# A two-layer hybrid trunk on one core: norms moved into a matmul group, a branch tile run ahead, and a re-laid end

## The chip, the core and the metric

The kernel runs on one core of a Trainium2 chip. The metric is the device time of one execution in microseconds (us); less is better. The median of the runs shown is 905.42 us (905.33 to 906.95, three runs).

Engines have short names, as in the profile: PE is TensorE (PEld its weight loads), DVE is VectorE, ACT is ScalarE, POOL is GpSimd, SP is the engine that only issues DMAs here. ACT issues some DMAs too. SPq and ACTq are the queues of these issues.

## The reference, cut to what matters

1024 prompt tokens and 32 tokens of a second stream go through two layers of width 1024. Layer 0 is a gated recurrence over 1408 channels, layer 1 a windowed attention, and each adds its normed output to its input:

```python
def rglru_block(x, ...):                      # layer 0
    u = rmsnorm(x, norm_pre) @ w_in           # 1024 -> 2 x 1408
    branch, gate = u[..., :D_RNN], u[..., D_RNN:]
    conv = conv_b + sum of four taps of branch along the tokens
    xb = conv in 16 blocks of 88 channels
    r = sigmoid(xb @ w_r + b_r)               # block-diagonal, 88 x 88
    i = sigmoid(xb @ w_i + b_i)
    h = recurrence(a(r), b(r, i, conv))       # along the tokens
    y = (h * silu(gate)) @ w_out
    return x + rmsnorm(y, norm_post)
k, v = shared_kv(x)                           # from the output of layer 0
def swa_block(x, k, v, ...):                  # layer 1
    u = rmsnorm(x, norm_pre) @ w_in           # queries and a gate
    o = windowed attention with sinks(q, k, v)
    y = (o * silu(gate)) @ w_out
    return x + rmsnorm(y, norm_post)
```

The outputs are y of both streams, the last rows of the convolution, the last states of the recurrence, and the K and V rows. The order of sums and the fp32 accuracy matter to the kernel only in that it computes every product of two fp32 matrices from halves, as follows.

## The kernel before, in words

**Products.** Every fp32 operand of a matmul is split into a high part (rounded to the matmul's format fp32r) and a low part (what is left). `split` (L112 to L117) makes them: ACT copies the high part (L116), and VectorE subtracts it (L117); for some weights GpSimd subtracts. `mm3` (L146 to L152) computes a product as three matmuls for each 128 rows of the inner dimension: high weights by high data (L150), high by low (L151), low by high (L152). An inner dimension of 1024 is thus a group of 24 matmuls, all added up in one PSUM bank. `mm3_steps` (L698) is the same as a generator that hands the control back every six matmuls, so that other work can be traced between. A bank holds 512 fp32 columns; eight banks go round.

**Tokens.** All tokens stand along the free dimension, 1060 columns with three columns of gap between the streams, in three chunks `NSA`: 0 to 384, 384 to 768, 768 to 1060. Channels stand along the 128 partitions: the 1408 branch channels are 11 tiles `br0` to `br10`.

**The front.** x arrives chunk by chunk. The first NS = 3 branch tiles are run chunk by chunk as well (`first_mm`, L310): tiles 0, 1, 2 of chunk 0, then of chunk 1, then of chunk 2 (loop at L328). `branch_mm` multiplies with x unnormed; the factor 1/rms of each token comes later. `x_stat(n)` makes it for three token tiles: ACT squares rows of x, small operations finish the root, and VectorE writes it on the diagonal of a 128 x 128 matrix `diag` (L289). `x_norm(n)` (L291 to L306) multiplies these by a matrix of ones (L296, banks `rs0` to `rs2`), which puts the factors on all partitions, and ACT copies them to `rs` (L299). Then come `branch_evac` (L207: VectorE, `ext` = bank times `rs`), and `branch_conv`: ACT does the first tap (L222), VectorE three more (L224, one operation each), and the result is split to `chi` and `clo`. In the loop, `x_norm(0)` is called behind tile 1 of chunk 1 and `x_norm(1)` behind tile 0 of chunk 2; `x_norm(2)` follows the loop.

**Branch and gates.** The loop at L445 goes over the branch tiles from 3 on: `branch_mm(t)` for all three chunks, `branch_evac`, the next weights, `branch_conv`, and then `gates` of an earlier tile by the table `GATES_AT`: gate 0 stands behind branch tile 3, gate 1 behind tile 4, and so on. A gate product (bank `gt<tile>_<gate>_<chunk>`) has the tile's own 128 channels and a few rows of its neighbours, since blocks of 88 channels cross the tiles. These rows are packed into a tile `pack` by DMAs (`pack_rows`, L371; half of them issued by SP, half by ACT), and each bank's group is closed by two matmuls with them (L390, L391). `weights` loads weight tiles through four buffers `raw` and splits them into six buffers each of `whi` and `wlo`.

**The order.** The program is traced as written, and a scheduler then orders each engine's instructions by a simulated time and by priorities. `urgent()` raises the priority of what is traced in it. `pin` keeps an instruction behind the one that was traced before it on the same engine; what isn't pinned may be moved ahead. A tile's buffers come free when the last reader has run, and the next load into the same buffer waits for that.

**The end.** `out_b(1)` projects the last-but-one group of tokens (416 columns, `OUT[1]`) onto eight tiles of channels, banks `obm0_1` to `obm7_1`. Each bank is read twice by ACT: the square `qp` (L614), which GpSimd adds to a running sum (L616), and the copy `zb`. When the eighth is added, `rsqrt_of` (L158, bank `ss_p`) multiplies the sum by ones on TensorE, and `post_norm` normalises the eight `zb` tiles on VectorE (L601), adds the residuals `res` (loaded by SP in 16 DMAs, L580; the addition is L607), and SP stores them. Meanwhile `prep_t(c, k)` (L1095 to L1104) loads and splits the sixteen weight tiles of the last product, `t<c>_<k>`: c is the half of the output channels, k the 128 rows of the inner dimension. They go through the same four `raw` buffers. `T_AT` places t0_0 to t0_7 and t1_6, t1_7 into `out_b(1)` (split to `wth`, `wtl`); t1_0 to t1_5 are traced at the start of `out_t` (split to `wthi`, `wtlo`, for they take the ring's buffers `whi`, `wlo`).

`out_t` (L1106 to L1149) computes the last 256 tokens the other way round: tokens on partitions, 512 output channels in a bank. There are four tiles in the order (c, t) = (0, 0), (0, 1), (1, 0), (1, 1), banks `ot<t>_<c>`, 24 matmuls each. For each ACT squares the bank with a running sum (`junk`, L1134) and VectorE multiplies the bank by the gain into `zt` (L1137). When both halves of a token tile are there, TensorE transposes the residual into the banks `xt` (L1125), a few operations on one column finish the root, VectorE does `zt` times root plus `xt` for each half (L1147), and two DMAs store them, the first issued by SP, the second by ACT. The loop at L1159 runs `out_t` and, behind each of its steps, one step of `norm_b(1)`, which is the norm of the eight `zb` tiles.

## Time and profile before

| what | before |
|---|---|
| median of the runs | 905.42 us (905.33 to 906.95) |
| the profiled execution's own time | 905.81 us |
| its span in the profile | 904.0 us |
| mean granted TensorE clock | 0.995 |
| PE busy from 0 to 75 us | 69.70 us, clock 0.98 |
| PE busy from 75 to 862 us | 782.14 of 787 us, clock 1.00 |
| PE busy from 862 to 890 us | 25.79 of 28 us, clock 0.94 |
| PE busy from 890 to 904 us | 7.72 of 14 us, clock 0.91 |

The profile is that of one execution; times in it count from the span's start. A row of a timeline gives start and length in us, the engine, the line, the operation with its tiles, shapes, how many of a kind follow each other (x6), and in brackets the idle time before it and what ended it. "PEclk" and the clock in a row of stretches are the TensorE clock that the chip granted, as a share of the full one. Durations of single matmuls overlap each other, so the cost of one is read from the distance between starts.

### The profile page before, as it was taken

The page shows a single profiled execution, that of the slowest core. Times are in us where ns is not written, and L with a number is a line of the kernel's source. Part 1 is how long each engine was busy: PE and PEld are TensorE (multiplying, and loading weights), DVE is VectorE, ACT ScalarE, POOL GpSimd, SP SyncE. Part 2 cuts the span into 40 slices and gives each one's busy share as a digit, 9 for nine tenths or more (in the row PEclk, how much of TensorE's full clock was granted, in tenths as well). Part 3 has the DMA queues.
Part 4 walks back from the last instruction along what each step waited for, and adds up shares of the span by engine and source line. Part 5 has one row for each costly group of instructions (what it writes and reads, how often), then busy time and mean ns, then how long its engine had stood idle before and what let it go on. Part 6 is the DMA issues. An engine that isn't in the chain of part 4 may idle for free. (4 is left out here: it accounts for less than half of the span.)

```text
span 904.0 us, 15787 instructions
## 1 busy us (share of the span) xinstructions
PE 885.4 (98%) x5434; PEld 864.4 (96%) x5434; DVE 708.1 (78%) x1499; ACT 563.1 (62%) x1231; POOL 221.7 (25%) x263
## 2 busy tenths in 40 slices
PE   9989999999999999999999999999999999999997
PEld 8989999999999999999989899999999999999975
DVE  6797878878897654177897847999999989998776
ACT  8748877879454325364663527766767757797661
POOL 5250212114300001126362432122122011202330
PEclk9999999999999999999999999999999999999999
DMA  9522433242533216445545667338338338334884
GB/s 337 204 75 77 135 88 125 81 128 92 181 119 124 89 57 190 146 135 178 163 157 186 210 205 205 98 111 231 96 110 239 103 97 239 121 112 160 281 250 144
DMA packets 95777, 137.35 MB, mean 152 GB/s; under 512 B 16144, under 2 KB 64304, under 8 KB 95696
## 3 DMA queue, kind: packets, MB, share of 16 engines
q1 hardware_dynamic: 86040, 123.30, 43.9%
q10 hardware_dynamic: 9480, 12.49, 4.5%
q8 instruction: 43, 0.70, 0.3%
q0 software_dynamic: 176, 0.54, 0.2%
q14 instruction: 38, 0.31, 0.1%
HBM read 99.28 MB, written 32.13 MB: 145 GB/s over the span
## 5 line engine op out<-in xcount | busy, mean ns | idle before, releaser
L150 PE MATMUL oa<-yh,whi_outa 128*128 128x384 f32 (+1 forms) x264 | 85.8, 326 | 0.0
L151 PE MATMUL gb<-xlo,whi_ina 128*128 128x384 f32 (+1 forms) x264 | 85.6, 324 | 0.0
L152 PE MATMUL gb<-xhi,wlo_ina 128*128 128x384 f32 (+1 forms) x264 | 85.4, 323 | 0.0
L150 PE MATMUL gb<-xhi,whi_ina 128*128 128x384 f32 (+1 forms) x264 | 85.2, 323 | 0.0
L151 PE MATMUL oa<-yl,whi_outa 128*128 128x384 f32 (+1 forms) x264 | 85.1, 323 | 0.0
L152 PE MATMUL oa<-yh,wlo_outa 128*128 128x384 f32 (+1 forms) x264 | 85.1, 323 | 0.0
L616 POOL TENSOR_TENSOR qp<-qp,qp 128x384 f32<-128x384 f32 (+2 forms) x34 | 49.3, 1449 | 138.2 <-ACT qp L614 126.5
L150 PE MATMUL br<-xhi,whi_ina 128*128 128x384 f32 (+1 forms) x240 | 77.8, 324 | 0.0
L151 PE MATMUL br<-xlo,whi_ina 128*128 128x384 f32 (+1 forms) x240 | 77.8, 324 | 0.0
L152 PE MATMUL br<-xhi,wlo_ina 128*128 128x384 f32 (+1 forms) x240 | 77.4, 323 | 0.0
L117 DVE TENSOR_TENSOR wlo_outa<-raw_outa,whi_outa 128x512 fp32r<-128x512 f32 (+1 forms) x60 | 43.7, 742 | 42.7 <-ACT whi_outa L116 42.6
L931 ACT ACTIVATE P<-P,sm 128x257 f32<-128x257 f32 (+1 forms) x132 | 64.3, 490 | 8.0 <-DVE sm L928 7.9
L698 PE MATMUL gB<-xl,whi_g 128*128 128x384 f32 (+1 forms) x192 | 63.0, 328 | 0.0
L698 PE MATMUL gB<-xh,whi_g 128*128 128x384 f32 (+1 forms) x192 | 62.9, 328 | 0.0
L698 PE MATMUL gB<-xh,wlo_g 128*128 128x384 f32 (+1 forms) x192 | 62.6, 326 | 0.0
L116 ACT ACTIVATE whi_outa<-raw_outa 128x512 fp32r<-128x512 f32 (+1 forms) x60 | 35.5, 594 | 41.5 <-PE oa L151 25.1
L224 DVE SCALAR_TENSOR_TENSOR conv<-ext,pa,conv 128x1060 f32<-128x1060 f32 (+2 forms) x51 | 50.2, 1005 | 9.0 <-ACT conv L222 8.6
L928 DVE CUSTOM_DVE_ANT_0 P<-S,mask,nsnk 128x256 f32<-128x256 f32 (+1 forms) x128 | 52.8, 463 | 4.9 <-PE S L926 4.8
L151 PEld LDWEIGHTS oa<-yl,whi_outa 128*128 128x128 f32 x264 | 49.6, 188 | 0.4
L150 PEld LDWEIGHTS oa<-yh,whi_outa 128*128 128x128 f32 x264 | 49.6, 188 | 0.4
L150 PEld LDWEIGHTS gb<-xhi,whi_ina 128*128 128x128 f32 x264 | 49.7, 188 | 0.0
L152 PEld LDWEIGHTS oa<-yh,wlo_outa 128*128 128x128 f32 x264 | 49.7, 188 | 0.0
(301 smaller groups left out, 2894.0 us busy)
## 6 DMA issues: line engine op xcount, KB each, us to landing
raw_ina<-w_in_a SPq DMA_DIRECT2D x44, 256.0 KB, 2.8
raw_outa<-w_out_a SPq DMA_DIRECT2D x40, 256.0 KB, 2.7
raw_ob<-w_out_b SPq DMA_DIRECT2D x32, 256.0 KB, 2.6
qscr<-quadq SPq DMA_DIRECT2D x8, 768.0 KB
Q<-qscr SPq DMA_DIRECT2D x32, 192.0 KB, 4.3
hscr<-u SPq DMA_DIRECT2D x11, 530.0 KB, 3.0
xr<-xr SPq DMA_DIRECT2D x8, 512.0 KB, 10.2
raw_g<-w_in_b SPq DMA_DIRECT2D x16, 256.0 KB, 3.3
```

What stands on the lines that cost most here:

```text
L116: pin(S.activation(dst_hi, src, AF.Copy), behind)
L117: (lo_eng or V).tensor_tensor(dst_lo, src, dst_hi.bitcast(F32), op=ALU.subtract)
L150: nc.tensor.matmul(ps, wh, xh, start=i == 0, stop=False)
L151: nc.tensor.matmul(ps, wh, xl, start=False, stop=False)
L152: nc.tensor.matmul(ps, wl, xh, start=False, stop=last and i == n - 1)
L224: V.scalar_tensor_tensor(c, e[:, c0 + k:c1 + k], pa[:, t, k:k + 1], c, op0=ALU.mult, op1=ALU.add)
L616: G.tensor_tensor(sums[0], sums[0], q, op=ALU.add)
L698: nc.tensor.matmul(ps, l, r, start=c == 0, stop=c == 3 * n - 1)
L928: V.tensor_tensor_reduce(pt[:, h, :w], sb[:, (h - h0) * 256:(h - h0) * 256 + w], msk, -0.125, nsnk[:, sk][:, h:h + 1], op0=ALU.add, op1=AL ...
L931: S.activation(pt[:, h, :w + 1], pt[:, h, :w + 1], AF.Exp, bias=nmax[:, h:h + 1], scale=-1.0, accum_out=rsum[:, h:h + 1])
```

## The change

It has five parts.

1. `mm3` gets two more arguments. `mid` is called when half of the groups' steps have been traced, and the matmul behind it is pinned; `behind` pins the first matmul. `branch_mm` and `first_mm` pass both on. In the front's loop `x_norm(n - 1)` is now called in the middle of the tile behind which it stood (tile 1 of chunk 1, tile 0 of chunk 2), and the first matmul of the tile that follows is pinned.
2. At t = 3, chunks 0 and 1 of branch tile 4 are multiplied and evacuated ahead of gate 0; at t = 4 only its chunk 2 is left.
3. In `prep_t` the split of the second half's weights (c = 1) is pinned on ACT behind what was traced before it.
4. The last tile of `out_t` (c = 1, t = 1) is computed in two half banks of 256 columns, each with its own square and gain; the first half's sum (`s2`) is added into `s0`.
5. The loop over `out_t` leaves out the step of `norm_b(1)` behind the first step of `out_t`.

```diff
-    def mm3(ps, ws, xs, last=True):
+    def mm3(ps, ws, xs, last=True, mid=None, behind=False):
         n = len(ws)
         for i, ((wh, wl), (xh, xl)) in enumerate(zip(ws, xs)):
-            nc.tensor.matmul(ps, wh, xh, start=i == 0, stop=False)
+            if mid and i == n // 2:
+                mid()
+            pin(nc.tensor.matmul(ps, wh, xh, start=i == 0, stop=False), behind and i == 0 or mid and i == n // 2)
...
     for n in (1, 2):
         for m in range(NS):
-            first_mm(n, m)
-            if m == 2 - n:
-                x_norm(n - 1)
+            first_mm(n, m, (lambda: x_norm(n - 1)) if m == 2 - n else None, m == 3 - n)
...
     for t in range(MR):
         if t >= NS:
-            branch_evac(t, branch_mm(t))
+            branch_evac(t, branch_mm(t, (2,) if t == 4 else (0, 1, 2)))
         wts.pop(t)
         if t >= NS - 2:
             prep_in(t + 2)
+        if t == 3:
+            branch_evac(4, branch_mm(4, (0, 1)))
...
-        split(*wt[c, k], raw)
+        split(*wt[c, k], raw, behind=c == 1)
...
         for c in range(2):
             for t in range(2):
...
+                s0, s1, ms, y, r, s2 = (sm[:, t, i:i + 1] for i in range(6))
+                parts = [(0, 256, s2), (256, 512, s1)] if c and t else [(0, 512, s1 if c else s0)]
+                for a, b, acc in parts:
+                    ps = bank(f"ot{t}_{c}_{a}")[:, :b - a]
+                    yield from mm3_steps(ps, [tuple(x[:, t * P:(t + 1) * P] for x in oghl[k, 2]) for k in range(KD)],
+                                         [tuple(x[:, a:b] for x in wt[c, k]) for k in range(KD)])
+                    junk = fin_tile(f"junk{t}_{c}_{a}", b - a, "junk", bufs=1)
+                    S.activation(junk, ps, AF.Square, accum_out=acc)
+                    if c == 0:
+                        V.tensor_scalar(s0, s0, 1.0 / 1024.0, EPS, op0=ALU.mult, op1=ALU.add)
+                    V.tensor_tensor(zt[t][:, c * 512 + a:c * 512 + b], ps, gpost[:, c * 512 + a:c * 512 + b], op=ALU.mult)
+                    if acc is s2:
+                        V.scalar_tensor_tensor(s0, s2, 1.0 / 1024.0, s0, op0=ALU.mult, op1=ALU.add)
...
-    for _ in out_t():
-        next(nb, None)
+    for i, _ in enumerate(out_t()):
+        if i:
+            next(nb, None)
```

How these parts move instructions in the engines' queues is shown at three places. A row of the order has the line, the operation, the tile written, the tiles read, the shape, how many alike follow each other, and in some lists the semaphores waited for. Lines below L146 of before are two to nine further down in the changed kernel.

The first place is TensorE's queue in the front, before: `br1_1` is tile 1 of chunk 1, `br2_1` tile 2 of chunk 1, `rs0` the bank of the first norm.

```order
L152 MATMUL br1_1_376<-xhi6_98,wlo_ina1_4_194 128x384
L150 MATMUL br1_1_376<-xhi7_99,whi_ina1_4_193 128x384
L151 MATMUL br1_1_376<-xlo7_107,whi_ina1_4_193 128x384
L152 MATMUL br1_1_376<-xhi7_99,wlo_ina1_4_194 128x384
L296 MATMUL rs0_401<-diag_141,ones_66 128x128
L150 MATMUL br2_1_436<-xhi0_92,whi_ina2_0_226 128x384
L151 MATMUL br2_1_436<-xlo0_100,whi_ina2_0_226 128x384
L152 MATMUL br2_1_436<-xhi0_92,wlo_ina2_0_227 128x384
L150 MATMUL br2_1_436<-xhi1_93,whi_ina2_0_226 128x384
L296 MATMUL rs0_401<-diag_141,ones_66 128x128 x2
```

The same place in the changed kernel:

```order
L152 MATMUL br1_1_376<-xhi3_95,whi_ina1_0_187 128x384
L153 MATMUL br1_1_376<-xlo3_103,whi_ina1_0_187 128x384
L154 MATMUL br1_1_376<-xhi3_95,wlo_ina1_0_188 128x384
L298 MATMUL rs0_389<-diag_141,ones_66 128x128 x3
L152 MATMUL br1_1_376<-xhi4_96,whi_ina1_4_193 128x384
```

All three matmuls of `rs0` stand together now, twelve matmuls ahead of the end of tile 1, where the first of them stood.

The second place is TensorE's queue where gate 0 begins, before (`br3_2` is the last chunk of branch tile 3, `gt0_0_2` is gate 0's first half, chunk 2):

```order
L151 MATMUL br3_2_736<-xlo7_107,whi_ina3_4_648 128x292
L152 MATMUL br3_2_736<-xhi7_99,wlo_ina3_4_649 128x292
L150 MATMUL gt0_0_0_799<-chi0_410,whi_gate0_0_654 128x384
L151 MATMUL gt0_0_0_799<-clo0_411,whi_gate0_0_654 128x384
L152 MATMUL gt0_0_0_799<-chi0_410,wlo_gate0_0_655 128x384
L150 MATMUL gt0_0_1_806<-chi0_410,whi_gate0_0_654 128x384
L151 MATMUL gt0_0_1_806<-clo0_411,whi_gate0_0_654 128x384
L152 MATMUL gt0_0_1_806<-chi0_410,wlo_gate0_0_655 128x384
L150 MATMUL gt0_0_2_813<-chi0_410,whi_gate0_0_654 128x292
L150 MATMUL gt0_1_0_821<-chi0_410,whi_gate0_0_654 128x384
```

And in the changed kernel (`br4_1` is chunk 1 of branch tile 4, `pack0` the packed rows):

```order
L152 MATMUL br4_1_803<-xhi7_99,whi_ina4_4_669 128x384
L153 MATMUL br4_1_803<-xlo7_107,whi_ina4_4_669 128x384
L154 MATMUL br4_1_803<-xhi7_99,wlo_ina4_4_670 128x384
L152 MATMUL gt0_0_0_853<-chi0_398,whi_gate0_0_654 128x384
L153 MATMUL gt0_0_0_853<-clo0_399,whi_gate0_0_654 128x384
L154 MATMUL gt0_0_0_853<-chi0_398,wlo_gate0_0_655 128x384
L390 MATMUL gt0_0_0_853<-pack0_658,whi_gate0_0_654 128x384
L391 MATMUL gt0_0_0_853<-pack0_658,wlo_gate0_0_655 128x384
```

The 48 matmuls of `br4_0` and `br4_1` stand ahead of gate 0, and the packed rows are asked for behind three matmuls of it; before, the scheduler had put matmuls of other banks ahead of the packed rows, the one that waits for chunk 2 (`gt0_0_2`) among them.

The third place is the end. ACT's queue around the last square, before (`qp4_1_7` is the square of the eighth bank, `wth1_7` and `wthi1_0` to `wthi1_4` are splits of the last weights; a name in the waits is a semaphore: DMAHW4 is signalled by a load):

```order
L116 ACTIVATE wth1_7_10677<-raw_t1_7_10675 128x512 [waits DMAHW7_49]
L614 ACTIVATE qp4_1_6_10623<-obm6_1_10597 128x416 [waits PE_49,Pool_49]
L1045 ACTIVATE zb6_1_10622<-obm6_1_10597,gains_82 128x416 [waits DVE_49]
L116 ACTIVATE wthi1_0_10720<-raw_t1_0_10718 128x512 [waits DMAHW0_49]
L116 ACTIVATE wthi1_1_10726<-raw_t1_1_10724 128x512 [waits DMAHW2_49]
L116 ACTIVATE wthi1_2_10732<-raw_t1_2_10730 128x512 [waits DMAHW3_49,DVE_49]
L116 ACTIVATE wthi1_3_10738<-raw_t1_3_10736 128x512 [waits DMAHW4_49,DVE_49]
L614 ACTIVATE qp4_1_7_10665<-obm7_1_10639 128x416 [waits PE_49]
```

ACT's queue in the changed kernel:

```order
L616 ACTIVATE qp4_1_6_10623<-obm6_1_10597 128x416 [waits PE_49,Pool_49]
L1047 ACTIVATE zb6_1_10622<-obm6_1_10597,gains_82 128x416 [waits DVE_49]
L116 ACTIVATE wthi1_0_10720<-raw_t1_0_10718 128x512 [waits DMAHW0_49]
L116 ACTIVATE wthi1_1_10726<-raw_t1_1_10724 128x512 [waits DMAHW2_49]
L116 ACTIVATE wthi1_2_10732<-raw_t1_2_10730 128x512 [waits DMAHW3_49,DVE_49]
L616 ACTIVATE qp4_1_7_10665<-obm7_1_10639 128x416 [waits PE_49]
L1047 ACTIVATE zb7_1_10664<-obm7_1_10639,gains_82 128x416
L116 ACTIVATE wth1_6_10671<-raw_t1_6_10669 128x512 [waits DMAHW4_49]
L116 ACTIVATE wth1_7_10677<-raw_t1_7_10675 128x512 [waits DMAHW7_49]
L116 ACTIVATE wthi1_3_10738<-raw_t1_3_10736 128x512 [waits DMAHW4_49,DVE_49]
```

The splits of t1_6, t1_7 and t1_3 have gone behind the last square; those of t1_0, t1_1 and t1_2 have not.

SP's queue at the same place, before (`raw_t1_2` is the load of weight tile t1_2, `res4_1_0` the first residual):

```order
L1098 DMA raw_t1_1_10724<-w_out_t 128x512 [waits DMAHW2_49,DVE_49]
L1098 DMA raw_t1_2_10730<-w_out_t 128x512 [waits DMAHW4_49,DMAHW3_49,DVE_49]
L1098 DMA raw_t1_3_10736<-w_out_t 128x512 [waits DMAHW7_49,DVE_49]
L1098 DMA raw_t1_4_10742<-w_out_t 128x512 [waits DMAHW5_49,DMAHW0_49,DVE_49]
L1098 DMA raw_t1_5_10748<-w_out_t 128x512 [waits DMAHW6_49,DMAHW2_49,DVE_49]
L580 DMA res4_1_0_10681<-x1scr_3742 128x384
```

SP's queue in the changed kernel:

```order
L1100 DMA raw_t1_2_10730<-w_out_t 128x512 [waits DMAHW3_49,DMAHW0_49,DVE_49]
L1100 DMA raw_t1_3_10736<-w_out_t 128x512 [waits DMAHW4_49,DMAHW2_49,DVE_49]
L582 DMA res4_1_0_10681<-x1scr_3742 128x384 [waits DMAHW5_49]
...
L582 DMA res4_1_7_10688<-x1scr_3742 128x32 [waits DMAHW4_49]
L1100 DMA raw_t1_4_10742<-w_out_t 128x512 [waits DMAHW5_49,DVE_49]
L1100 DMA raw_t1_5_10748<-w_out_t 128x512 [waits DMAHW6_49,DVE_49]
L1059 DMA o_y<-zb0_1_10250 128x416 [waits DMAHW7_49,DVE_49]
```

The load of t1_2 waits for DMAHW0 in place of DMAHW4, which the load of t1_0 and that of t1_6 signal: it takes the buffer that t1_0 frees, where it took t1_6's. The loads of t1_4 and t1_5 have gone behind the sixteen residual loads. On ACT's queue the store of the first token tile's second half (`o_yt` from `zt0`) now stands ahead of the last square.

More of the change, by code (lines that the diff above doesn't have):

```diff
@@ L189, in _trunk, with branch_mm @@
     conv, chl, ext, gw, pack = {}, {}, {}, {}, {}
-    def branch_mm(t, ns=(0, 1, 2)):
+    def branch_mm(t, ns=(0, 1, 2), mid=None, behind=False):
         if t not in ext:
@@ L198, in branch_mm @@
             ps = bank(f"br{t}_{n}")
-            mm3(ps[:, :c1 - c0], wts[t], x_of(c0, c1))
+            mm3(ps[:, :c1 - c0], wts[t], x_of(c0, c1), mid=mid, behind=behind)
             banks.append((n, ps))
@@ L308, in _trunk, with first_mm @@
     open_ = {0: [], 1: [], 2: []}
-    def first_mm(n, m):
+    def first_mm(n, m, mid=None, behind=False):
         if n == 0 and m:
             prep_in(m)
-        open_[n].append(branch_mm(m, (n,)))
+        open_[n].append(branch_mm(m, (n,), mid, behind))
     x_split(0)
@@ L1128, in out_t @@
             for t in range(2):
-                ps = bank(f"ot{t}_{c}")
-                yield from mm3_steps(ps, [tuple(x[:, t * P:(t + 1) * P] for x in oghl[k, 2]) for k in range(KD)],
-                                     [wt[c, k] for k in range(KD)])
-                junk = fin_tile(f"junk{t}_{c}", 512, "junk", bufs=1)
-                s0, s1, ms, y, r = (sm[:, t, i:i + 1] for i in range(5))
-                S.activation(junk, ps, AF.Square, accum_out=s1 if c else s0)
-                if c == 0:
-                    V.tensor_scalar(s0, s0, 1.0 / 1024.0, EPS, op0=ALU.mult, op1=ALU.add)
-                V.tensor_tensor(zt[t][:, c * 512:(c + 1) * 512], ps, gpost[:, c * 512:(c + 1) * 512], op=ALU.mult)
+                s0, s1, ms, y, r, s2 = (sm[:, t, i:i + 1] for i in range(6))
[11 more added lines that the diff above has]
+                        V.scalar_tensor_tensor(s0, s2, 1.0 / 1024.0, s0, op0=ALU.mult, op1=ALU.add)
                 if c == 1:
```

## The prediction

> **What bounds the kernel now.** I read the page first: the engine shares, then TensorE's waits, then its stretches and its timeline at the two long waits.
>
> ```profile
> span 904.0 us, 15787 instructions
> PE 885.4 (98%) x5434; PEld 864.4 (96%) x5434; DVE 708.1 (78%) x1499; ACT 563.1 (62%) x1231; POOL 221.7 (25%) x263
> ```
>
> TensorE is the bound: 904.0 - 885.4 = 18.6 us is all the time that a reordering can win from its idle time. The change removes no matmul, so I look for where those 18.6 us lie.
>
> ```profile
> PE gt L150 <- ACT chi L116: 3.6, 1, 3.6
> PE ss_p L158 <- POOL qp L616: 2.2, 1, 2.2
> PE rAk L698 <- DVE xl L117: 1.8, 2, 1.3
> ```
>
> The two longest single waits are one in the front (a gate matmul waits for the split of the third chunk, 3.6 us) and one at the end (the ones-matmul ss_p waits for the last sum of squares, 2.2 us). The change touches both. The stretches show what such a wait costs besides itself (columns: start and end, length, busy time of PE, PEld, DVE, ACT, POOL, then TensorE's granted clock, DMA share, GB/s).
>
> ```profile
> 60.00:65.00 5.00, 2.81 (x9) 2.81 (x10) 5.00 (x11) 1.79 (x4) 3.12 (x2) 0.67 0.30 84
> 500.00:600.00 100.00, 96.83 (x625) 93.76 (x624) 76.24 (x204) 54.82 (x153) 30.84 (x32) 1.00 0.51 156
> 878.00:880.00 2.00, 2.00 (x6) 1.57 (x5) 1.97 (x5) 0.77 (x3) 0.00 (x0) 0.50 0.84 234
> ```
>
> After the 3.6 us wait and after the 2.2 us wait the granted clock was low (0.67, 0.50); in the stretch that holds the 1.3 us wait it was 1.00. So a wait of 2.2 us or more is paid twice, one of 1.3 us once.
>
> **The front.** TensorE's timeline (start, length):
>
> ```profile
> 29.64 0.38 PE L296 MATMUL rs<-diag,ones 128*128 128x128 f32 x2
> ...
> 44.84 0.94 PE L296 MATMUL rs<-diag,ones 128*128 128x128 f32 x6
> ...
> 57.38 0.33 PE L150 MATMUL gt<-chi,whi_gate 128*128 128x384 f32 x1
> ...
> 58.26 0.33 PE L152 MATMUL gt<-chi,wlo_gate 128*128 128x384 f32 x1
> 62.19 0.93 PE L150 MATMUL gt<-chi,whi_gate 128*128 128x292 f32 x2 [3.60 <-ACT chi L116]
> ...
> 65.47 0.34 PE L150 MATMUL br<-xhi,whi_ina 128*128 128x384 f32 x1
> ...
> 70.51 0.34 PE L152 MATMUL br<-xhi,wlo_ina 128*128 128x384 f32 x1
> 70.97 0.41 PE L390 MATMUL gt<-pack,whi_gate 96*128 96x384 f32 x1
> ```
>
> One 384-column matmul takes (58.26 - 57.38) / 5 = 0.176 us from start to start, one of 292 columns by its columns 0.134. The stretch loses three things: 62.19 - 58.26 - 0.176 = 3.75 us of standing; then the six matmuls of 384 and six of 292 columns from 62.19 to 65.47 take 3.28 us where 6 x 0.176 + 6 x 0.134 = 1.86 would do, so 1.42 us of low clock; and 70.97 - 70.51 - 0.176 = 0.28 us for the packed rows. Together 5.45 us, the most that the front can win.
>
> Now 48 matmuls of branch tile 4 (two chunks of 384) stand ahead of the first gate matmul: 48 x 0.176 = 8.4 us of work that needs only x and weights that were split by 50 us. Gate 0 then starts at 57.38 + 8.4 = 65.8. What it waited for must be ready by then. These are the engines that feed it:
>
> ```profile
> 25.48 0.68 DVE L289 TENSOR_SCALAR diag<-ident,stat 128x128 f32<-128x128 f32 x3
> ...
> 31.73 1.49 DVE L207 TENSOR_TENSOR ext<-br,rs 128x384 f32<-128x384 f32 x3 [1.82 <-ACT rs L299]
> ...
> 44.08 4.28 DVE L224 SCALAR_TENSOR_TENSOR conv<-ext,pa,conv 128x384 f32<-128x384 f32 x4
> ...
> 49.85 2.73 DVE L224 SCALAR_TENSOR_TENSOR conv<-ext,pa,conv 128x384 f32<-128x384 f32 x5
> ...
> 62.92 1.19 DVE L117 TENSOR_TENSOR clo<-conv,chi 128x292 fp32r<-128x292 f32 x3
> ```
> ```profile
> 44.57 1.28 POOL L117 TENSOR_TENSOR wlo_ina<-raw_ina,whi_ina 128x512 fp32r<-128x512 f32 x1 [2.23 <-ACT whi_ina L116]
> ```
> ```profile
> 63.39 2.83 SPq L371 DMA_DIRECT2D pack<-clo  x3
> ```
> ```profile
> DMA to landing us min/median/max: 6.5/6.5/6.5
> ```
>
> The splits end at 62.92 + 1.19 = 64.1 already today, 1.7 us before 65.8, so the 3.75 us and their 1.42 us of low clock go even if VectorE gains nothing. The packed rows are the next thing late: 63.39 is their issue, about 64.4 that of tile 1's part, and with 6.5 us to landing they came at 70.9, just when TensorE took them. In the new order TensorE wants them after three matmuls of gate 0, at 65.8 + 0.5 = 66.3. With the old issue it would stand 70.9 - 66.3 = 4.6 us there.
>
> ```profile
> 31.20 0.49 ACT L299 ACTIVATE rs<-rs 128x384 f32<-128x384 f32 x1 [1.50 <-PE rs L296]
> ```
>
> So the other front edit carries weight: x_norm(0) in the middle of a tile. The three rs matmuls stood in two pieces, the first behind tile 1; now all three stand twelve matmuls earlier, at 29.64 - 12 x 0.176 = 27.5. Their input is there at 25.48 + 0.68 = 26.2, so the pin makes no wait. With some 0.6 us for the three (0.94 for three at 44.84) and ACT's 0.49 they let VectorE's ext start near 28.7, which is 3.0 us sooner than 31.73, and VectorE was idle then. How much of it lasts? Its convs take 4.28 / 4 = 1.07 us each beside POOL's weight splits and 2.73 / 5 = 0.55 without, and convs moved forward meet more of POOL's splits. Bounds: nothing lasts (0), or 5 us do (chunk 1's norm comes forward too). I take 3.3, near the 3 of the start. Then the packed rows land at 70.9 - 3.3 = 67.6, less the 0.4 below: TensorE stands 0.9 us, inside the range that costs no clock. The whole-bank norms of chunk 2 at 44.84 are pinned as before and need a diag that VectorE now makes among those slow convs; I put 0.4 us for it (0 to 1). It delays everything behind it, gate 0 too, which is why it comes off the landing's lateness.
>
> The front: 5.45 - 0.4 - 0.9 + about 0.2 for the fewer changes between rs and branch matmuls = 4.4 us won; range 5.4 to 2.0. Branch 4's last chunk needs the bank of its first, which VectorE frees behind the first conv of tile 3, some 4 us before TensorE asks. From 75 us on TensorE shows no wait for hundreds of us and ACT's work after gate 0 shifts as well, so I let the gain stand to the end.
>
> **The end.** ACT, POOL, TensorE, VectorE and the DMA queue at the 2.2 us wait:
>
> ```profile
> 872.09 1.70 ACT L116 ACTIVATE wthi<-raw_t 128x512 fp32r<-128x512 f32 x3
> 874.65 0.63 ACT L116 ACTIVATE wthi<-raw_t 128x512 fp32r<-128x512 f32 x1 [0.86 <-DMA raw_t<-w_out_t]
> 875.18 0.50 ACT L614 ACTIVATE qp<-obm 128x416 f32<-128x416 f32 x1
> ```
> ```profile
> 875.82 1.10 POOL L616 TENSOR_TENSOR qp<-qp,qp 128x416 f32<-128x416 f32 x1 [2.85 <-ACT qp L614]
> ```
> ```profile
> 871.33 0.69 DVE L117 TENSOR_TENSOR wtl<-raw_t,wth 128x512 fp32r<-128x512 f32 x1 [1.08 <-ACT wth L116]
> ```
> ```profile
> 874.52 7.54 SPq L580 DMA_DIRECT2D res<-x1scr  x16
> ```
>
> The last square (875.18) stands behind a weight split that waits for its load. That load (t1_3) could start only when VectorE had split t1_7 and freed its buffer, 871.33 + 0.69 = 872.0, and took until 874.65: 2.6 us. The pin moves the splits of t1_6 and t1_7 behind the square, but those of t1_0, t1_1 and t1_2 stay ahead, as the order shows, and t1_2 now takes t1_0's buffer. So the square waits for t1_0's landing, its two splits, and t1_2's load. t1_0 is issued right behind t1_7, which landed near 870.7 (VectorE's split at 871.33 follows ACT's 0.63 us one), and it was there by 872.09; I take 871.2 (bounds 870.7 and 872.1). Splits 0.63 + 0.69 give 872.6, the load 2.6 gives 875.2, the split about 0.55 until the next starts: the square at 875.7, 0.5 us later than now (bounds 0 and 1.4). The wait for ss_p does not go; it grows by about 0.5, less 0.2 for the two transposes that stand ahead of it now.
>
> The loads t1_4 and t1_5 fall behind the sixteen residual loads.
>
> ```profile
> res<-x1scr SPq DMA_DIRECT2D x6, 192.0 KB, 2.9
> ```
> ```profile
> 887.74 0.40 PE L698 MATMUL ot<-wthi,ogh 128*128 128x512 f32 x1
> ```
> ```profile
> 880.82 1.09 DVE L601 TENSOR_TENSOR zb<-zb,r 128x416 f32<-128x416 f32 x2
> ...
> 890.16 1.09 DVE L607 TENSOR_TENSOR zb<-zb,res 128x416 f32<-128x416 f32 x2
> ```
>
> SP starts the residuals about 0.8 us sooner (t1_3 waits for t1_1's splits, near 873.3), so t1_4 is issued near 873.7 + 7.54 = 881.3 and lands with about 3 us, as the residuals do (2.9), at 884.4. Split, it is ready at 884.4 + 0.63 + 0.69 = 885.7. TensorE takes it at 887.74 now and some 0.4 us later then, so it has 2.4 us of cover. But VectorE's zb work stands behind that split, in order. Its first three operations would be done near 883.4 (1 us later than from 880.82), it idles until 885.0, and it has two splits to do there (1.4 us). Its list, done at 890.16 + 1.09 = 891.2 now, is done near 893.4. From there the tail follows:
>
> ```profile
> 896.89 0.60 ACT L1134 ACTIVATE junk<-ot 128x512 f32<-128x512 f32 x1 [4.80 <-DMA o_yt<-zt]
> ...
> 897.61 0.69 DVE L1137 TENSOR_TENSOR zt<-ot,gpost 128x512 f32<-128x512 f32 x1 [2.72 <-ACT junk L1134]
> ...
> 899.29 1.41 DVE L1147 SCALAR_TENSOR_TENSOR zt<-zt,smt,xt 128x512 f32<-128x512 f32 x2
> ```
>
> ```profile
> L117 DVE TENSOR_TENSOR ogl<-ogr,ogh 128x256 fp32r<-128x256 f32 x6 | 2.5, 416 | 0.0
> ```
>
> With half a bank last, the square and the gain after the last matmul shrink as a 256-column operation does (0.42 us against 0.69): some 0.25 us each, 0.5 won. The 48 half-width matmuls cost what 24 cost, by columns. But tile 0's output DMA on ACT's queue now stands ahead of the last square and waits for VectorE, which comes late: I put 0.6 lost (0 to 2). The end: +0.3 - 0.5 + 0.6 = 0.4 us lost; range 0.7 won to 2 lost.
>
> **Sum.** The profiled execution took 905.81 us (904.0 of span). 905.81 - 4.4 + 0.4 = 901.8. The median of the runs, 905.42, lies 0.39 below, so I predict 901.4 for a median. A difference under 0.2% (1.8 us) can't be told from none.
>
> **The rule weighed.** Row: the 2.2 us wait was followed by a granted clock of 0.50. The Trainium skill, "TensorE: Matmul & The Clock Gate", "Why this matters for your kernels", says to leave no idle gap over about 3 us between bursts. By that rule a 2.2 us gap would keep the clock. This trace disagrees (0.50 in the row), and the measurement decides. It matters for the first rival, where a pack wait of 2.2 to 3 us is paid with the low clock by the rows; by the page's rule its time would be 1.4 us less, 903.8.
>
> **Rivals.**
> - *The packed rows take the wait's place* (or the gain is given back in a later wait for VectorE). For it: 4.6 us of lateness if VectorE gains nothing. Against: its 1.82 us idle before ext. With 3 us of wait the low clock returns: 5.45 - 0.4 - 3.0 - 1.4 = 0.6 won, 0.4 lost at the end: 905.2 as a median.
> - *The end's wait does go*, if t1_2's load comes early. For it: 2.2 and about 1.4 us of clock are there. Against: the square still stands behind t1_2. 901.4 - 3.6 = 897.8.
> - *Slower: t1_4 lands late behind the residual loads.* Each us of lateness goes through VectorE's list to the end, and past 2.4 us TensorE stands too. A full queue is in this profile:
>
> ```profile
> xr<-xr SPq DMA_DIRECT2D x8, 512.0 KB, 10.2
> ```
>
>  With 10.2 instead of 3 us: 7.2 later, 908.6. It decides for slower from 4.0 + 1.8 = 5.8 us of lateness. Against: the residual loads' own landing is near 3.
>
> **How the numbers follow.** Forecast 0.63, packed rows or given back 0.20, end's wait goes 0.10, late t1_4 0.07. The forecast's bounds, front and end both best or both worst, are 905.4 - 5.4 - 0.7 = 899.3 and 905.4 - 2.0 + 2.0 = 905.4; the first rival's 905.2 belongs inside. So 899.0 to 905.6 leaves out the second rival and the third, 0.17. Faster by over 0.2% is below 903.6: 0.61 of the forecast and the 0.10, so 0.71. Within: 0.02 and nearly all of the 0.20, 0.21. Slower: 0.07 and a little, 0.08.
>
> **What would show it.** Right: no wait at gt0 near 62; rs near 27.5; a wait under 1.3 us at the first pack matmul; clock 1.00 there; the ss_p wait still 2 us or more with its low clock; the last square right behind tile 0's output DMA. Wrong: a pack wait over 2 us, an ss_p without wait, VectorE waiting past 888 for t1_4.

## The result, and the profile after

The changed kernel takes 901.35 us (median of 11 runs, 900.23 to 905.13), the kernel before, run beside it, 905.94 us (11 runs). The ratio is 0.9950, with a 95% interval of 0.9936 to 0.9964: faster by 3.3 to 5.8 us. The forecast was 901.4 us.

The profiled execution of the changed kernel is a long one, 903.26 us. First the head of its page, then TensorE's waits in the front and at the end (in all, times, longest).

```profile
span 901.5 us, 15838 instructions
PE 881.8 (98%) x5458; PEld 863.3 (96%) x5458; DVE 704.3 (78%) x1501; ACT 563.9 (63%) x1233; POOL 214.0 (24%) x263
```
```profile
PE br L152 <- ACT xhi L120: 1.5, 2, 0.8
...
PE rs L298 <- DVE diag L291: 0.3, 1, 0.3
```
```profile
PE ss_p L160 <- POOL qp L618: 1.4, 1, 1.4
```

The 3.6 us wait of the gate matmul is gone, a wait of 0.3 us at the norms of chunk 2 is new, and the ss_p wait is 1.4 us instead of 2.2. The stretches of the changed kernel, in the same columns as before:

```profile
60.00:65.00 5.00, 5.00 (x31) 5.00 (x30) 2.68 (x7) 3.07 (x5) 3.04 (x5) 1.00 0.63 149
65.00:70.00 5.00, 5.00 (x32) 5.00 (x31) 4.23 (x5) 2.33 (x4) 0.00 (x0) 1.00 0.40 122
...
876.00:878.00 2.00, 2.00 (x10) 1.65 (x9) 1.97 (x5) 0.57 (x2) 0.00 (x0) 1.00 0.84 237
```

TensorE is busy through the stretch that held the gate's wait, and the clock is 1.00 there and behind the ss_p wait; before it was 0.67 and 0.50. The front in the timelines of TensorE, VectorE, GpSimd and SP, and the landing of the packed rows:

```profile
28.25 0.83 PE L298 MATMUL rs<-diag,ones 128*128 128x128 f32 x6
...
67.20 0.34 PE L154 MATMUL gt<-chi,wlo_gate 128*128 128x384 f32 x1
67.37 0.34 PE L390 MATMUL gt<-pack,whi_gate 96*128 96x384 f32 x1
...
74.95 0.34 PE L152 MATMUL gt<-chi,whi_gate 128*128 128x384 f32 x1
```
```profile
42.99 3.75 DVE L291 TENSOR_SCALAR diag<-ident,stat 128x128 f32<-128x128 f32 x3
...
59.57 1.20 DVE L117 TENSOR_TENSOR clo<-conv,chi 128x292 fp32r<-128x292 f32 x3
```
```profile
44.18 2.53 POOL L117 TENSOR_TENSOR wlo_ina<-raw_ina,whi_ina 128x512 fp32r<-128x512 f32 x2
```
```profile
60.05 4.20 SPq L371 DMA_DIRECT2D pack<-clo  x3
```
```profile
DMA to landing us min/median/max: 5.3/5.3/5.3
```

The row at 74.95 is the first matmul of gate 1. Up to there both kernels have done the same matmuls, so it is a milestone; before it stood here:

```profile
79.36 0.34 PE L150 MATMUL gt<-chi,whi_gate 128*128 128x384 f32 x1
```

The front won 79.36 - 74.95 = 4.4 us in these two executions, the sum of the prediction. The end, in ACT's and VectorE's timelines:

```profile
868.22 0.63 ACT L116 ACTIVATE wthi<-raw_t 128x512 fp32r<-128x512 f32 x1 [0.32 <-DMA raw_t<-w_out_t]
869.36 0.63 ACT L116 ACTIVATE wthi<-raw_t 128x512 fp32r<-128x512 f32 x1 [0.51 <-DMA raw_t<-w_out_t]
872.41 0.63 ACT L116 ACTIVATE wthi<-raw_t 128x512 fp32r<-128x512 f32 x1 [2.42 <-DMA raw_t<-w_out_t]
872.95 0.50 ACT L616 ACTIVATE qp<-obm 128x416 f32<-128x416 f32 x1
...
882.12 0.63 ACT L116 ACTIVATE wthi<-raw_t 128x512 fp32r<-128x512 f32 x1 [5.55 <-DMA raw_t<-w_out_t]
...
894.38 0.34 ACTq L1156 DMA_DIRECT2D o_yt<-zt  x1
894.82 0.38 ACT L1140 ACTIVATE junk<-ot 128x256 f32<-128x256 f32 x1 [4.31 <-DVE zt L1155]
```
```profile
882.79 0.69 DVE L117 TENSOR_TENSOR wtlo<-raw_t,wthi 128x512 fp32r<-128x512 f32 x1 [2.31 <-ACT wthi L116]
...
892.94 1.41 DVE L1155 SCALAR_TENSOR_TENSOR zt<-zt,smt,xt 128x512 f32<-128x512 f32 x2
895.33 0.42 DVE L1143 TENSOR_TENSOR zt<-ot,gpost 128x256 f32<-128x256 f32 x1 [0.99 <-ACT junk L1140]
```

The last square `qp` (872.95) stands behind the split of t1_2, which waits 2.42 us for its load. VectorE waits 2.31 us for the late t1_4. And the last square of all (894.82) stands behind the output DMA of tile 0 (894.38) on ACT's queue, which waits for VectorE; the last matmul had started at 892.47.

### The profile page after: what moved, and what is told of

Read it like the earlier page. It is cut to its first block, busy times and chain, and to the rows that moved or that the text cites. A ratio compares the mean times of both kernels' runs of the same rounds, so it can differ in the third digit from the quotient of the medians.

```text
span 901.5 us, 15838 instructions
## 1 busy us (share of the span) xinstructions
PE 881.8 (98%) x5458; PEld 863.3 (96%) x5458; DVE 704.3 (78%) x1501; ACT 563.9 (63%) x1233; POOL 214.0 (24%) x263
## 5 line engine op out<-in xcount | busy, mean ns | idle before, releaser
L618 POOL TENSOR_TENSOR qp<-qp,qp 128x384 f32<-128x384 f32 (+2 forms) x34 | 45.2, 1331 | 142.1 <-ACT qp L616 116.5
L117 DVE TENSOR_TENSOR wlo_outa<-raw_outa,whi_outa 128x512 fp32r<-128x512 f32 (+1 forms) x60 | 45.7, 773 | 42.3 <-ACT whi_outa L116 42.2
L116 ACT ACTIVATE whi_outa<-raw_outa 128x512 fp32r<-128x512 f32 (+1 forms) x60 | 35.3, 594 | 39.9 <-PE oa L153 25.0
L226 DVE SCALAR_TENSOR_TENSOR conv<-ext,pa,conv 128x1060 f32<-128x1060 f32 (+2 forms) x51 | 46.2, 925 | 10.7 <-ACT conv L224 10.2
```

The source lines that it names most:

```text
L116: pin(S.activation(dst_hi, src, AF.Copy), behind)
L117: (lo_eng or V).tensor_tensor(dst_lo, src, dst_hi.bitcast(F32), op=ALU.subtract)
L226: V.scalar_tensor_tensor(c, e[:, c0 + k:c1 + k], pa[:, t, k:k + 1], c, op0=ALU.mult, op1=ALU.add)
L618: G.tensor_tensor(sums[0], sums[0], q, op=ALU.add)
```

## The experiments

Two theories stood against each other at the start. Theory: the front won its 4 to 5 us, and the end gave nothing. Rival: the front wins less in the long run, since the profiled execution lost 2.8 us between gate 1 and the first ot matmul, and the end won 0.9 us. The marks of all runs are gathered in one table: the start of gate 1, the time from there to the first matmul of `out_t`, from there to the start of its last one, from that to the end of the span (the tail), and the ss_p wait. Each is from TensorE's timeline and the span of the one profiled execution. The next column is the median of the times, and the last the ratio to runs of the kernel before on the same chip, with its interval. The kernel before had medians of 904.92 to 906.37 us on these chips, so kernels are better compared by the ratio than by the median.

```
kernel                    gate1  middle  out_t  tail  ss_p  median  ratio (95%)
before                    79.36  789.33  27.76  7.55  2.2   905.94
changed                   74.95  792.14  25.38  9.03  1.4   901.35  0.9950 (0.9936-0.9964)
e1 front edits            73.73  792.08  25.84  7.55  1.9   901.09  0.9954 (0.9937-0.9970)
e2 end edits              78.85  789.21  25.61  9.83  1.7   907.72  1.0029 (1.0012-1.0046)
e3 branch 4 ahead         78.77  790.87  25.00  7.76  1.0   903.73  0.9987 (0.9967-1.0006)
e4 norms in the middle    75.35  791.59  25.05  7.61  1.2   901.02  0.9954 (0.9930-0.9979)
e5 changed, no pin        73.79  789.17  25.54  7.40  1.5   899.57  0.9942 (0.9926-0.9959)
e6 changed, whole bank    73.50  791.89  25.31  9.40  1.4   901.88  0.9970 (0.9956-0.9984)
e7 changed, DMA on SP     74.20  791.99  25.30  8.51  1.3   900.93  0.9960 (0.9946-0.9973)
e8 built, norms only      75.53  791.71  24.29  7.07  0.2   899.30  0.9940 (0.9926-0.9953)
e9 before again           78.68  794.69  25.78  7.55  1.8   908.55  (one run)
e10 built, both           73.64  790.53  24.13  7.40  -     897.76  0.9916 (0.9898-0.9935)
```

**e1: the front edits alone.** Against the changed kernel:

```diff
-        split(*wt[c, k], raw, behind=c == 1)
+        split(*wt[c, k], raw)
...
-                parts = [(0, 256, s2), (256, 512, s1)] if c and t else [(0, 512, s1 if c else s0)]
+                parts = [(0, 512, s1 if c else s0)]
...
-        if i:
-            next(nb, None)
+        next(nb, None)
```

> The two front edits alone (norms in the middle of a tile, branch tile 4 ahead), the end as before. Theory: the front carries the change. The first gate matmul is at 66 to 67 us, the packed rows make no wait of over 1 us, gate 1 begins 4.4 to 5.1 us sooner than in the kernel before (79.36 there), and the time falls by 4.0 to 5.0 us. The ss_p wait at the end is 2 us or more, as before. Rival: the 2.8 us that the changed kernel's profiled execution lost between gate 1 and the first ot matmul are a cost of the shifted front (a gain given back in the attention stages). Then the first ot matmul comes only 1.6 us sooner than 868.69 here too, and the time falls by about 2 us.

Its 901.09 us are the changed kernel's time: the front carries the change. Gate 1 began 5.6 us sooner than in the kernel before, more than the 4.4 to 5.1 expected, and the ss_p wait was 1.9 us, just under the 2 expected. The first ot matmul came at 865.81, 2.9 us sooner than 868.69 and not only 1.6, but the middle did take 2.75 us longer than in the first profile of before. Whether that is a price of the front or chance was left to e9.

**e2: the end edits alone.** The front is as before:

```diff
-            first_mm(n, m, (lambda: x_norm(n - 1)) if m == 2 - n else None, m == 3 - n)
+            first_mm(n, m)
+            if m == 2 - n:
+                x_norm(n - 1)
...
-            branch_evac(t, branch_mm(t, (2,) if t == 4 else (0, 1, 2)))
+            branch_evac(t, branch_mm(t))
...
-        if t == 3:
-            branch_evac(4, branch_mm(4, (0, 1)))
```

> The three end edits alone (split of the last weights pinned, last tile in two half banks, one step of the norm left out), the front as before. Theory from the two traces: from the first ot matmul to the end of the span it took 35.3 us before and 34.4 us after, so the end alone wins about 0.9 us, with a ss_p wait of 1.3 to 1.6 us and a clock of 1.00 behind it, and the last square waits for the output DMA on ACT's queue. Rival, the prediction's own step: the end loses 0.4 us, because the ss_p wait stays at 2 us or more and VectorE's list is late.

Slower, by 1.1 to 4.2 us. Both numbers missed; the sign is the prediction's, the size is larger. The profiled execution is one of e2's shortest, 905.25 us. ACT's timeline shows what it loses at the end:

```profile
891.26 0.39 ACT L1140 ACTIVATE junk<-ot 128x256 f32<-128x256 f32 x1 [0.68 <-PE ot L700]
...
896.29 0.34 ACTq L1156 DMA_DIRECT2D o_yt<-zt  x1
896.74 0.38 ACT L1140 ACTIVATE junk<-ot 128x256 f32<-128x256 f32 x1 [5.00 <-DVE zt L1155]
```

ACT stood 5.0 us before the last square, while the last matmul had started at 893.67. The tail is 9.83 us instead of 7.55, and from the first ot matmul to the end it took 35.4 us, the changed kernel 34.4. The parts do not add up well: by the ratios e1 wins 4.2 us and e2 loses 2.6, while both together win 4.5. Why the end edits cost more behind the old front was not tried.

**e3: branch tile 4 ahead alone.** The norms are as before, and so is the end (the three hunks of e1):

```diff
-            first_mm(n, m, (lambda: x_norm(n - 1)) if m == 2 - n else None, m == 3 - n)
+            first_mm(n, m)
+            if m == 2 - n:
+                x_norm(n - 1)
```

> Branch tile 4 ahead of gate 0 alone; the norms stand behind their tiles as before, and the end is as before. Theory (the prediction's step): the splits are no longer waited for, but the packed rows land near 70.9 us as before, so TensorE stands 4 to 5 us at the first packed matmul, the clock falls behind that, and the time is within 1 us of the kernel before. Rival: the gate's wait was the whole of it, the rows come earlier as well because ACT and SP issue them sooner, and the time falls by over 3 us.

As the theory had it in kind, with less lateness than the 4 to 5 us: no wait for the splits, but one of 3.2 us for the packed rows, and the low clock behind it. The median is 1.9 us below that of the kernel before, not within 1 us, but the interval of the ratio includes no change.

```profile
PE gt L392 <- DMA pack<-clo: 3.2, 1, 3.2
```
```profile
65.00:70.00 5.00, 1.84 (x7) 1.56 (x6) 3.64 (x4) 2.92 (x3) 0.00 (x0) 0.74 0.46 137
70.00:75.00 5.00, 5.00 (x20) 5.00 (x20) 0.70 (x1) 1.89 (x4) 0.00 (x0) 0.58 0.00 0
```

Gate 1 began at 78.77, between the 79.36 and 78.68 of the two profiles of before. This is the first rival of the prediction: the packed rows take the wait's place. It holds for this edit without the other.

**e4: the norms in the middle of a tile alone.** Gate 0 is ahead of branch tile 4 as before, and the end is as before (the three hunks of e1):

```diff
-            branch_evac(t, branch_mm(t, (2,) if t == 4 else (0, 1, 2)))
+            branch_evac(t, branch_mm(t))
...
-        if t == 3:
-            branch_evac(4, branch_mm(4, (0, 1)))
```

> The norms in the middle of a tile alone; gate 0 stands ahead of branch tile 4 as before, and the end is as before. Theory A: with VectorE 3.3 us sooner the gate's wait at chunk 2 falls from 3.6 to about 0.4 us, its low clock goes with it, and the packed rows are asked for among branch tile 4; the time falls by 3.5 to 5 us, nearly as much as with both edits, so branch tile 4 ahead is worth under 1 us. Theory B (both edits are needed): TensorE reaches the wait or the packed rows sooner too and stands 2 us or more somewhere before gate 1; the time falls by 1 to 3 us.

Theory A, in the time: 901.02 us, as much as both edits. The gate's wait is gone, and a small one for the packed rows is left:

```profile
64.53 0.44 PE L390 MATMUL gt<-pack,whi_gate 96*128 96x384 f32 x1 [0.66 <-DMA pack<-clo]
```

By the milestone branch tile 4 ahead still adds something. Gate 1 began at 75.35 here (75.53 in e8), and at 73.50 to 74.95 in the six executions with both edits: 1.5 us sooner in the mean (73.97 against 75.44), more than the theory's "under 1". The medians of e1 and e4 do not show these 1.5 us; e10 and e8, which differ by branch tile 4 too, stand 1.5 us apart with intervals that overlap.

**e5, e6, e7: the end taken apart.** Each is the changed kernel with one line undone or moved.

e5:

```diff
-        split(*wt[c, k], raw, behind=c == 1)
+        split(*wt[c, k], raw)
```

e6:

```diff
-                parts = [(0, 256, s2), (256, 512, s1)] if c and t else [(0, 512, s1 if c else s0)]
+                parts = [(0, 512, s1 if c else s0)]
```

e7:

```diff
-                        (nc.scalar if i else nc.sync).dma_start(A["o_yt"][t][:, i * 512:(i + 1) * 512], z)
+                        (nc.scalar if i and t else nc.sync).dma_start(A["o_yt"][t][:, i * 512:(i + 1) * 512], z)
```

> The changed kernel without the pin on the last weights' splits; both front edits, the half banks and the left-out step stay. Theory: the pin is what costs at the end, because it lets the loads of t1_4 and t1_5 fall behind the sixteen residual loads and so makes VectorE's list late. Without it VectorE's list is done before the last matmul, tile 0's output DMA is issued before the last square is ready, and the half bank saves its 0.5 us: from the first ot matmul to the end 32 to 33 us (34.4 with the pin, 33.4 with the front edits alone), a time of 900.0 to 900.8, some 0.5 to 1.5 us below the changed kernel and 5 to 6 us below the kernel before. Rival: the half banks cost, and the tail behind the last matmul stays at 9 us (9.0 in the changed kernel, 7.55 in the kernel before).

> The changed kernel with the last tile in one whole bank; the pin, the left-out step and both front edits stay. Theory: VectorE's list is late as in the changed kernel, so the tail behind the last matmul stays at 8.5 us or more, and from the first ot matmul to the end it takes 34.4 us or a little more; the time is within 0.5 us of the changed kernel. Rival: the half banks are what costs (a second square behind the output DMA on ACT's queue); then the tail falls to 7.6 us and the time by 1.0 to 1.5 us.

> The changed kernel with both output DMAs of token tile 0 issued by SP, none by ACT. Theory: the last square no longer waits behind the DMA of tile 0 (idle of 4.3 us on ACT, 0.99 us on VectorE in the changed kernel): it starts right behind the last matmul, VectorE works through without the 0.99 us, and the time falls by 0.7 to 1.0 us against the changed kernel. Rival: VectorE's list alone sets the end and the DMA's place costs nothing; then the tail stays at 9.0 us.

e5 came out as the theory had it in the trace: without the pin the tail is 7.40 us. Its median, 899.57, lies a little below the 900.0 to 900.8 expected, and its interval overlaps the changed kernel's. ACT's timeline shows the DMA of tile 0 issued 2 us ahead of a square that then waits for the matmul:

```profile
886.88 0.34 ACTq L1156 DMA_DIRECT2D o_yt<-zt  x1
888.88 0.38 ACT L1140 ACTIVATE junk<-ot 128x256 f32<-128x256 f32 x1 [2.34 <-PE ot L700]
```

e6 keeps the pin and keeps a long tail, 9.40 us, as expected; its median is 0.5 us above the changed kernel's, at the edge of what was expected. So the pin costs 1.6 us of tail with half banks (9.03 against 7.40), and the half banks save 0.4 (9.03 against 9.40). Against e1's 7.55 the pin costs 1.9 with a whole bank and the half banks save 0.2, but these two pairs also differ by the left-out step of `norm_b(1)`, which no run undoes alone. In e7 the last square comes at once, but VectorE's late list stays, and half a microsecond of the tail goes, not 0.7 to 1.0; the median, 900.93, cannot be told from the changed kernel's.

```profile
891.87 0.38 ACT L1140 ACTIVATE junk<-ot 128x256 f32<-128x256 f32 x1 [2.34 <-PE ot L700]
```
```profile
892.55 1.41 DVE L1155 SCALAR_TENSOR_TENSOR zt<-zt,smt,xt 128x512 f32<-128x512 f32 x2
```

**e8 and e10: a version built from these.** Four of the splits stand ahead of the last square and only those of t1_2 to t1_5 are pinned behind it; all the loads are traced ahead of the residuals. e8 has the norms of e4 in the front, e10 both front edits.

```diff
-    T_AT = ((), (), (), (0, 1), (2, 3), (4, 5), (6, 7), (14, 15))
+    T_AT = ((), (), (), (0, 1), (2, 3), (4, 5), (6, 7, 14, 15, 8, 9), (10, 11, 12, 13))
...
-        split(*wt[c, k], raw, behind=c == 1)
+        split(*wt[c, k], raw, behind=c == 1 and 2 <= k < 6)
...
-        for k in range(6):
-            prep_t(1, k)
...
-                        (nc.scalar if i else nc.sync).dma_start(A["o_yt"][t][:, i * 512:(i + 1) * 512], z)
+                        (nc.scalar if i and t else nc.sync).dma_start(A["o_yt"][t][:, i * 512:(i + 1) * 512], z)
```

> A version built from the runs so far: the norms in the middle of a tile, gate 0 ahead of branch tile 4 as in the kernel before, half banks, both output DMAs of token tile 0 on SP; the splits of t1_0, t1_1, t1_6 and t1_7 stand ahead of the last square, those of t1_2 to t1_5 are pinned behind it, and all six loads stand ahead of the residual loads. Theory: the last square no longer waits for the load of t1_2 and the ss_p wait falls under 0.5 us, with no low clock; VectorE's list is done before the last matmul; the tail is near 7.0 us. From the first ot matmul to the end about 31 to 32 us, so 1 to 2 us less than with the norms alone (901.02): 899.0 to 900.2. Rival: the late loads of t1_2 to t1_5 make VectorE or TensorE wait in the second half, and the time is 901 or more.

> The built version of the last job with both front edits (branch tile 4 ahead of gate 0 as well). Theory: by the traces branch tile 4 ahead takes gate 1 from 75.4 us to 73.5 to 74.2 us on top of the norms; the end is as in the built version (ss_p wait under 0.5 us, 31.4 us from the first ot matmul). So 1.2 to 1.8 us less than its 899.3: 897.5 to 898.2. Rival: what the front wins beyond 4 us is given back in later waits, as the equal medians of the norms alone and of both front edits (901.02 and 901.09) suggest; then 899 to 900.

Both came out inside the theory's range. The ss_p wait is 0.2 us in e8, and e10 shows none. e10's ACT timeline:

```profile
867.94 0.63 ACT L116 ACTIVATE wthi<-raw_t 128x512 fp32r<-128x512 f32 x1 [1.14 <-DMA raw_t<-w_out_t]
868.48 0.50 ACT L616 ACTIVATE qp<-obm 128x416 f32<-128x416 f32 x1
...
869.36 1.92 ACT L116 ACTIVATE wthi<-raw_t 128x512 fp32r<-128x512 f32 x3
```

The last square stands behind two early splits only. e10, 897.76 us, beats both kernels: its interval, 0.9898 to 0.9935, lies just below the changed kernel's, 0.9936 to 0.9964.

**e9: the kernel before, unchanged, for a second profile.**

> The kernel before, unchanged, for a second profile of it. Theory: the front's wait and what follows it are fixed by the order, so gate 1 begins at 78.8 to 79.5 us again and the gate's wait is 3.5 to 3.7 us; the ss_p wait at the end hangs on when a load lands and moves between executions (1.0 to 1.9 us in four kernels with the same order at the end), so the granted clock behind it falls to 0.50 only if the wait is over 2 us. Then the stretch from the first ot matmul to the end is 33 us with a short wait and 35.3 us with a long one. Rival: 2.2 us of wait and 35.3 us are typical for this kernel, and it is the earlier front that shortens them.

The theory held, but for 0.1 us of gate 1. The gate's wait is 3.6 us again and gate 1 begins at 78.68. The ss_p wait is 1.8 us this time, and the clock stays:

```profile
PE ss_p L158 <- POOL qp L616: 1.8, 1, 1.8
```
```profile
881.00:883.00 2.00, 1.74 (x7) 1.26 (x8) 1.70 (x4) 1.61 (x4) 0.20 (x1) 1.00 0.87 241
```

From the first ot matmul it took 906.7 - 873.37 = 33.3 us, 2 us less than in the first profile. And its middle took 794.69 us, 5.4 us more than in the first profile of the very same kernel. e5, with both front edits, took 789.17. So the 2.8 us of middle that the changed kernel lost are within what executions of one kernel differ by, and no price of the front shows in them: over the four kernels with the old front the middle took 791.0 us in the mean, over the six with both edits 791.3. TensorE's waits in the middle add up to 4.9 us in the first profile of before and to 8.7 in e9. They are small ones at many places, these three among them in e9:

```profile
PE rAk L698 <- DVE wlo_kA L121: 1.8, 2, 1.5
...
PE obm L698 <- DVE wlo_ob L117: 1.3, 2, 1.1
PE T L951 <- DVE P L943: 1.0, 2, 0.6
```

What decides them in an execution was not tried and stays open. In e1, e4 and e7 the middle also holds 3.4 us at a clock of 0.50, behind a wait of 1.4 us (last section).

## Why the prediction was right

The number was right, 901.4 against 901.35, and so were the mechanism and the sign of the front. Its size came out somewhat larger, and the end had two steps that failed; these errors fell on opposite sides. That the forecast met the median to 0.05 us is luck.

- *The gate's wait and its low clock go.* Right in every kernel with both front edits.
- *A wait of 2.2 us or more is paid twice, one of 1.3 us once.* So it was with the gate's waits and with ss_p. As a rule for any wait it fails: a wait of 1.4 us was followed by the low clock in e1 and e4 (last section).
- *VectorE gains 3.3 us.* Its splits ended at 60.77 instead of 64.11: 3.3 us in this pair of profiles, and more in the mean. The first norm was forecast at 27.5 and stood at 27.01 in e1. In the changed kernel it stood at 28.25, since that execution began with longer waits for x (1.5 us against 0.6) and with 3.4 us at the low clock, which the second of these rows shows; the first and the third are e1's:

```profile
27.01 0.83 PE L298 MATMUL rs<-diag,ones 128*128 128x128 f32 x6
```
```profile
8.60:11.80 3.20, 3.20 (x9) 2.84 (x10) 3.20 (x8) 3.20 (x7) 2.67 (x6) 0.50 1.05 386
```
```profile
58.33 1.20 DVE L117 TENSOR_TENSOR clo<-conv,chi 128x292 fp32r<-128x292 f32 x3
```

Over the six executions with both edits the splits ended at 59.8 in the mean, over the three with the old front (before, e2, e9) at 63.9: 4.1 us, inside the bounds of 0 and 5. The hit of 3.3 is one late execution's.
- *The norms carry the weight, since the rows would be 4.6 us late without them.* Right, and stronger than put: e3 shows the row wait (3.2 us), e4 that the norms alone win as much in the median. What the prediction did not see is how little branch tile 4 adds: 1.5 us at gate 1 to the 3.5 that the norms win alone (78.96 against 75.44). It credited the pair with the 5.45 us and never asked what the norms would do alone.
- *The packed rows wait 0.9 us.* No wait. The rows took 5.3 us from issue to landing here, by the profile, and 4.2 to 5.4 in the other five kernels with both edits, where 6.5 was taken from before; and VectorE's gain was larger in the mean. With branch tile 4 behind gate 0 (e4) they were there at 64.5. This term was mis-sized by 0.9 us.
- *The norms of chunk 2 cost 0.4 us.* The wait was 0.34, and as forecast their `diag` is slow beside GpSimd's splits: 3.75 us for three beside GpSimd's splits (the 2.53 us row and the one ahead of it), where the first three took 0.68 at 25.48 in the kernel before.
- *The front's 4.4 us.* 4.4 in the two profiles, where the late start and the missing wait for the rows nearly cancelled. Over the six executions with both edits gate 1 began at 73.97 in the mean, over the three with the old front at 78.96: 5.0 us, inside the 2.0 to 5.4.
- *The wait for ss_p does not go; it grows by about 0.5.* The first half is right, and the reason too: the square stays behind t1_2's split and its load. The second half failed, and with it the low clock that was to stay: it did not come in any kernel with the pin. With the pin the wait was 1.3 to 1.7 us in four kernels, without it 1.0 to 2.2 in six, so it did not grow. The step that failed is the landing of t1_0, put 2.5 us behind the first ot matmul (871.2 against 868.69); ACT took it 1.1 us behind it (868.22 against 867.09). From there to the square it took 4.7 us, where 4.5 was forecast, so the rest of the chain was right. And the 2.2 us to which the 0.5 was added were the longest of six waits with that order; one profile of before could not show it.
- *The tail: 0.5 saved by the half bank, 0.6 lost to the late list.* The sign is right, the size not: 9.03 us of tail against 7.55 is 1.5 lost in all. The late load, the delayed list and the DMA ahead of the last square are there as forecast: t1_4 was taken 15.0 us behind the first ot matmul, where 15.7 was forecast. The half bank saves 0.2 to 0.4 of the 0.5 forecast, and the lateness, put at 0.6, costs 1.6 to 1.9, near its outer bound of 2; in e2 the tail is 2.3 us longer than before.

So the end lost more than the 0.4 of the sum. Against the end stages of e1, e3, e4 and e9, which have the old order and no low clock (32.7 to 33.4 us), the changed kernel's 34.4 is 1.0 to 1.7 us worse, and e2's 35.4 is 2.1 to 2.8 worse. Against the one profile of before, 35.3 us with 1.9 us of long wait and low clock in it, it looked 0.9 better. The front in turn won 5.0 rather than 4.4 in the mean. 5.0 less some 1.4 is 3.6, inside the measured 3.3 to 5.8; with e2's end it would be 2.2 to 2.9, below it, and this stays open.

Of the rivals, the first comes true where the norms stay where they were (e3). The second, the ss_p wait gone, needs another order (e8, e10). The third, slower by a late t1_4, is what the pin does in small: 1.6 to 1.9 us, not 7, too little to turn the sum, though e2, without the front, is slower.

## What to carry to other kernels

Before work is moved into a wait, ask what feeds the waiter: here a norm traced twelve matmuls earlier took the wait away at its source, and the filler alone only moved the wait to the next late thing, the packed rows. A pin on one engine moves the loads of that engine's operands on another queue; read where the DMAs land in the order before counting the gain. And take a second profile of the kernel before: a wait that hangs on a load's landing was 2.2 us in one execution and 1.8 in the next, and only the first was followed by the low clock.

## What the runs showed of the hardware

Long waits cost clock in every case here, and some short ones did too. TensorE's waits of 1.0, 1.2, 1.3, 1.4, 1.4, 1.5, 1.7, 1.8 and 1.9 us for ss_p left the granted clock at 1.00; those of 2.2 us (before), 3.2 us (e3) and 3.6 us (before, e2, e9) were followed by 0.50 for 3.4 us, in e3 for 6.8. But no length of a wait parts the two. At its first matmuls into the bank `rAk` TensorE waits for the split `wlo_kA`, in the changed kernel and in e4 for the same 1.38 us:

```profile
463.27 0.44 PE L700 MATMUL rAk<-xh,wlo_kA 128*128 128x384 f32 x1 [1.38 <-DVE wlo_kA L121]
```
```profile
463.69 0.44 PE L698 MATMUL rAk<-xh,wlo_kA 128*128 128x384 f32 x1 [1.38 <-DVE wlo_kA L121]
```

Behind it the clock stayed at 1.00 in the changed kernel and fell to 0.50 in e4 (the stretch from 465 to 466 us of both):

```profile
465.00:466.00 1.00, 0.94 (x4) 0.47 (x3) 1.00 (x3) 0.53 (x2) 0.80 (x1) 1.00 0.00 0
```
```profile
465.00:466.00 1.00, 1.00 (x4) 1.00 (x5) 1.00 (x2) 0.86 (x3) 0.92 (x2) 0.50 0.00 0
```

e1 and e7 fell as e4 did (1.36 and 1.37 us), e8 stayed (1.38). Within each execution all the changes of the clock in the trace lie a whole number of 3.41 us apart (in e1 at 463.75, 467.16 and 897.24 us), so where a wait falls on that grid may decide; no run varied it alone. The Trainium skill, "TensorE: Matmul & The Clock Gate", "What's actually happening", puts the loss of the clock at an idle window of about 3.4 us. These runs show it behind waits of 1.4 to 2.2 us already, and the measurement decides.

Between gate 1 and the first ot matmul two profiles of one kernel differed by 5.4 us, with the same instructions in the same order, while the first 386 us of that stretch agreed within 0.15 us in all twelve profiles.
